# A hand-set order for the first 80 microseconds of a two-layer diffusion trunk

## The chip, the cores and the metric

The kernel runs on one core of one Trainium2 chip. The metric is device time in microseconds (us) for one launch; the time of a kernel is the median of its runs.

## The reference

Two layers work on 512 latent tokens `x` and 256 context tokens `ctx`, each token 1024 wide, all in float32. Only the start matters here:

```python
mod_x = split(silu(c) @ ada_w[0] + ada_b[0], 6)        # shift, scale, gate, ... for x
mod_c = split(silu(c_ctx) @ ada_w[0] + ada_b[0], 6)    # the same for ctx
h_x = rmsnorm(x, norm_g[0, 0]) * (1 + mod_x[1]) + mod_x[0]
h_c = rmsnorm(ctx, norm_g[0, 0]) * (1 + mod_c[1]) + mod_c[0]
p_x, p_c = h_x @ w_in, h_c @ w_in                      # q, k, v of 16 heads in 8 units
q, k = rope(q_x), rope(k_x)                            # latent tokens only
# then scores, softmax, values; output projection; SwiGLU FFN; layer 1; final RMSNorm
```

`rmsnorm(x, g)` is `x * rsqrt(mean(x * x) + eps) * g` over the 1024 features.

## The kernel before

Activations lie transposed: features on the 128 partitions, eight tiles `k = 0..7` of 128 features, tokens along the free dimension. A latent tile is 128x512, a context tile 128x256. Each float32 operand of a large product is split in two parts that TensorE takes at full rate, a high part (rounded by ScalarE) and a low part (the rest, by VectorE); a product is three matmuls, high by high, high by low and low by high (`mm3`). Weights arrive as raw tiles of 128x1024 (512 KB). The class `Stream` holds a list of them in order of use: `S.add` appends, `S.request` issues the loads on SyncE's queue (SP), `S.make` has the parts made, `S.next` hands them out. The pool of raw tiles has three buffers, one more pool at the start ("ada") five; a load waits until its buffer is free.

The start, up to the first attention scores, consists of these steps:

- Loads of `c` (`craw`), of the eight x tiles, and of `c` and `c_ctx` as rows (`crow`); silu of both on ScalarE (the rows are stored again, to be used later).
- The modulation. `ada_w` for shift and scale of the first norm comes in sixteen pieces, eight for features 0 to 511 and eight for 512 to 1023. TensorE multiplies each piece as four small products side by side (`ada_mm`). The sums are copied to SBUF, transposed by TensorE and added to the bias (`ada_out`), which gives `mod` (shift) and `amod` (gain times 1 + scale).
- 1/rms of x: ScalarE squares the tiles, VectorE and GpSimd add the squares into two accumulators (`sq_sum`), TensorE multiplies these with a matrix of ones, and ScalarE and VectorE make the inverse root (`rstd_of`).
- `h_make`: for a tile, VectorE computes x times `amod` times 1/rms, ScalarE adds the shift and rounds (the high part), VectorE makes the low part.
- `part(range(4))`: k, q and V products of unit 0 over tiles 0 to 3; then the second half of the modulation, and `part(range(4, 8))`. The weights are w_ab[8] (k), w_ab[0] (q), w_ab[12] and w_ab[13] (two halves of V).
- The context: its 1/rms, its eight tiles by `h_make`, its k, q and V products (`qk_c`, `v_group`).
- Rope on latent q and k (`rope_of`: a shuffle and a product on VectorE, a product and a sum on GpSimd); evacuation of q and k in two parts for two heads (`evac_pair`); and for k a second tile, k2, in which the halves of the partitions are swapped by two DMAs (`swap_halves`). Scores need k, k2 and q.

`keep_busy` issues small matmuls of `ident` by `ones`, whose results nobody uses.

The order of instructions on each engine is made by the tile framework's planner, which simulates the program and issues on each engine what is ready, in order of program text; `issue_after` pins single instructions. The planner places the loads and parts of later units among all this as buffers become free. Behind the first scores follow five steps of attention for each of eight units, with the projections of the next unit between them as fillers, and then the rest of the two layers.

Of the kernel before, what the change touches and what calls it, by code (L numbers as in the profile page):

```python
# [8 lines left out]
F32 = mybir.dt.float32  # L9
# [23 lines left out]
def f32(ap):  # L33
    return ap.bitcast(F32)
# [3 lines left out]
def tile_trunk(  # L38
# [53 lines left out]
    silu0 = nc.scalar.activation(csil, craw, AF.Silu)  # L92
# [202 lines left out]
    nc.sync.dma_start(tables[0:2, :], crow)  # L295
    with tc.issue_after(silu0.ins):
        silu1 = nc.scalar.activation(tables[0:2, :], tables[0:2, :], AF.Silu)
    nc.sync.dma_start(crow_dram, tables[0:2, :])
    exp_ln_tables(silu1)

# [7 lines left out]
    def rstd_of(ps, accs, dim, pool):  # L308

        n = accs[0].shape[-1]  # L310
        for i, a in enumerate(accs):
            nc.tensor.matmul(ps[:, 0:n], ones, a, start=i == 0, stop=i == len(accs) - 1)
        v = pool.tile([P, n], F32, tag="ns_v", name="ns_v")
# [314 lines left out]
    with ExitStack() as st:  # L628
# [24 lines left out]

        add_ada0(0)
        add_qk(0)
        S.add(w_ab[12])
        add_ada0(1)
        S.add(w_ab[13])
# [6 lines left out]
        with ExitStack() as s0:  # L665
            p0 = s0.enter_context(tc.tile_pool(name="p0", bufs=1, reuse_waits="tile"))
            p1 = PoolMap(ns_v=(p0, "ns_v", 1), ns_y=(p0, "ns_yc", 1), ns_t=(p0, "ns_t", 1))
            S.pools["ada"] = s0.enter_context(tc.tile_pool(name="p0_ada", bufs=5, reuse_waits="tile"))
            S.request(KT)
            nc.gpsimd.dma_start(cost, rope[0, 0])  # L670
            nc.gpsimd.dma_start(sint, rope[0, 1])

            def ada0_mm(b):
                ps = tp()
                for k in range(KT):
                    ada_mm(ps, S.next(0), k, k == 0, k == KT - 1)
                    S.request(min(S.at + 8, 2 * KT + 3))
                return ps

            def ada0_h(b, ps):  # L680
                sb = p0.tile([P, NX], F32, tag="ns_s", name="ada_acc", bufs=2)[:, 0:256]
                nc.vector.tensor_copy(sb, ps[:, 0:256])
                ada_out(sb, tp, [(0, 2, 0, 0, 4 * b), (2, 2, 0, 1, 4 * b)])
                for k in range(4 * b, 4 * b + 4):
                    h_make(k, hx[k], xr[k], rx, 0, 0, 0, p0)

            ps = ada0_mm(0)
            rx = rstd_of(tp(), sq_sum(xr, p0), D, p0)
            ada0_h(0, ps)
            keep_busy(tp(), 10)  # L690
            wk, wq, wv = S.next(), S.next(), S.next()
            psk, psq = linp(), linp()
            psv = [sp2((P, 2, 512)) for _ in range(2)]
            wv = [tuple(wslice(t, 256) for t in wv)]

            def part(ks):
                for ps, w in ((psk, wk), (psq, wq)):
                    wh, wl = (wslice(t) for t in w)
                    for k in ks:
                        nc.tensor.matmul(ps, wh(k), xh(k), start=(k == 0), stop=False)  # L700
                        nc.tensor.matmul(ps, wh(k), xl(k), start=False, stop=False)
                        nc.tensor.matmul(ps, wl(k), xh(k), start=False, stop=(k == KT - 1))
                for t in range(4):
                    c = slice(t * P, (t + 1) * P)
                    for k in ks:
                        wh, wl = wv[k // 4][0](k % 4), wv[k // 4][1](k % 4)
                        a, b = hx[k][:, 0, c], hx[k][:, 1, c]
                        nc.tensor.matmul(psv[t // 2][:, t % 2, 0:256], a, wh, start=(k == 0), stop=False)
                        nc.tensor.matmul(psv[t // 2][:, t % 2, 0:256], b, wh, start=False, stop=False)
                        nc.tensor.matmul(psv[t // 2][:, t % 2, 0:256], a, wl, start=False, stop=(k == KT - 1))  # L710

            for k in range(0, KT, 2):
                nc.sync.dma_start(c2[k // 2].rearrange("p (a b) -> p a b", a=2), ctxT[:, k : k + 2, :])
            part(range(4))
            rc = rstd_of(tp(), sq_sum(cr, p0), D, p1)
            for k in range(4):
                h_make(k, hc[k], cr[k], rc, 0, 0, 1, p0)
            ada0_h(1, ada0_mm(1))
            keep_busy(tp(), 9)
            wv.append(tuple(wslice(t, 256) for t in S.next()))  # L720
            part(range(4, KT))
            for k in range(4, KT):
                h_make(k, hc[k], cr[k], rc, 0, 0, 1, p0)
            del S.pools["ada"]
# [1258 lines left out]
```

## Time and profile before

| | |
|---|---|
| runs of the kernel | 1609.46, 1604.99, 1601.09 us |
| median | 1604.99 us |
| span of the profiled execution, first to last instruction | 1606.8 us |
| mean granted TensorE clock | 0.991 |
| share of the span in which PE, PEld, DVE, ACT, POOL are busy | 96%, 86%, 77%, 46%, 17% |
| first score on PE | 80.23 us after the start |

The page gives the profiled execution by its span alone; it lies between the times of the three runs. In a row of a timeline stand start, duration, engine (PE is TensorE's matmul, PEld its weight load, DVE is VectorE, ACT ScalarE, POOL GpSimd, SP SyncE; a q behind the name is the engine's queue of DMA issues), line in the kernel, operation, what is written from what, shape, count, and in brackets the idle time before it and what ended that. A float32 product with `ones` or `ident` counts as two records. The ends of matmuls are modelled and overlap; the distance of their starts is the time of one.

### The profile page before, as it was taken

How to read it: one execution, taken by the hardware profiler on the slowest of the kernel's cores; microseconds unless marked ns; L12 is line 12 of the kernel's file. 1: busy time of each engine (PE TensorE's matmuls, PEld its weight loads, DVE VectorE, ACT ScalarE, POOL GpSimd, SP SyncE). 2: the span in 40 equal slices, each digit the busy share in tenths (PEclk: the TensorE clock that was granted, in tenths of full speed). 3: DMA queues.
4: the chain of work that ended last, by engine and by line, in shares of the span. 5: the costliest groups of instructions: out<-in, count | busy, mean ns of one | idle time of the engine just before them, and what ended most of it. 6: DMA issues, size and time to landing. Idle time of an engine off the chain costs nothing.

```text
span 1606.8 us, 25479 instructions
## 1 busy us (share of the span) xinstructions
PE 1541.8 (96%) x9854; PEld 1377.4 (86%) x9854; DVE 1242.9 (77%) x2125; ACT 734.1 (46%) x1276; POOL 275.9 (17%) x311
## 2 busy tenths in 40 slices
PE   5899999999999999999999999999998999999997
PEld 3798888877878998999999998886777899989897
DVE  4667798966698789879798867677766987869686
ACT  4346545445344413434424254466664543525354
POOL 2222223463010000010100001354331000000001
PEclk9999999999999999999999999999999999999999
DMA  9312354543145465485866652320011442423321
GB/s 348 100 53 70 99 157 136 182 128 101 63 132 158 118 173 155 133 221 154 213 183 162 201 146 71 106 66 27 15 40 54 131 144 68 131 72 100 118 80 53
DMA packets 68577, 195.28 MB, mean 122 GB/s; under 512 B 6772, under 2 KB 19220, under 8 KB 68456
## 3 DMA queue, kind: packets, MB, share of 16 engines
q1 hardware_dynamic: 58824, 161.26, 31.5%
q0 software_dynamic: 9056, 31.87, 9.4%
q8 instruction: 78, 1.28, 0.3%
q10 hardware_dynamic: 576, 0.52, 0.1%
q14 instruction: 43, 0.35, 0.1%
HBM read 160.45 MB, written 4.86 MB: 103 GB/s over the span
## 4 chain that ended last, share of the span: by engine, by line
PE 52%; DVE 5%; DMA 4%; issue 4%; ACT 1%; POOL 0%; DVEq 0%; POOLq 0%; ACTq 0%; SPq 0%
PE f L1764 4%; PE f L1763 4%; PE f L1762 4%; PE f L1334 4%; PE f L1333 4%; PE f L1332 4%; PE f L1374 3%; PE f L1375 3%; PE f L1373 3%; PE t L411 2%; PE f L1815 2%; PE f L1817 2%; PE f L1816 2%; DMA wl<-raw 2%; PE t L1569 2%
## 5 line engine op out<-in xcount | busy, mean ns | idle before, releaser
L196 ACT ACTIVATE wh<-raw 128x1024 fp32r<-128x1024 f32 (+1 forms) x96 | 92.3, 978 | 232.4 <-DVE raw L540 106.6
L207 PE MATMUL lin<-hb,wh 128*128 128x512 f32 (+1 forms) x456 | 162.1, 356 | 8.3 <-DVE rbuf L387 2.1
L208 PE MATMUL lin<-hb,wh 128*128 128x512 f32 (+1 forms) x456 | 160.3, 351 | 1.0 <-DVE hb L1106 0.7
L209 PE MATMUL lin<-hb,wl 128*128 128x512 f32 (+1 forms) x456 | 158.4, 347 | 0.0
L197 DVE TENSOR_TENSOR wl<-raw,wh 128x1024 fp32r<-128x1024 f32 (+1 forms) x96 | 107.1, 1122 | 36.3 <-ACT wh L196 34.3
L269 DVE SCALAR_TENSOR_TENSOR junk<-raw,tables 128x1024 bf16<-128x1024 f32 x80 | 98.6, 1233 | 19.2 <-DMA raw<-in_ada_wT_dram 18.7
L202 POOL DMA_DIRECT2D wl<-raw x39 | 34.0, 872 | 445.3 <-ACT wl L201 412.0
L207 PEld LDWEIGHTS lin<-hb,wh 128*128 128x128 f32 x456 | 86.3, 189 | 23.9 <-issue 2.8
L1373 PE MATMUL f<-g,wh 128*128 128x512 f32 (+1 forms) x304 | 103.0, 340 | 0.6 <-DVE s L1362 0.6
L1374 PE MATMUL f<-g,wh 128*128 128x512 f32 (+1 forms) x304 | 102.9, 339 | 0.0
L1763 PE MATMUL f<-hb,wh 128*128 128x256 f32 x360 | 101.8, 284 | 0.0
L1762 PE MATMUL f<-hb,wh 128*128 128x256 f32 x360 | 101.6, 283 | 0.0
L1764 PE MATMUL f<-hb,wl 128*128 128x256 f32 x360 | 101.4, 284 | 0.0
L1375 PE MATMUL f<-g,wl 128*128 128x256 f32 (+1 forms) x304 | 100.8, 337 | 0.0
L1334 PE MATMUL f<-hb,wl 128*128 128x384 f32 x288 | 96.5, 335 | 1.0 <-DMA wl<-raw 1.0
L208 PEld LDWEIGHTS lin<-hb,wh 128*128 128x128 f32 x456 | 86.5, 190 | 12.4 <-DVE hb L1106 1.4
L159 DVE TENSOR_TENSOR wl<-raw,wh 128x1024 fp32r<-128x1024 f32 x61 | 80.7, 1325 | 20.6 <-ACT wh L158 20.3
L1332 PE MATMUL f<-hb,wh 128*128 128x384 f32 x288 | 96.4, 335 | 0.0
L1333 PE MATMUL f<-hb,wh 128*128 128x384 f32 x288 | 96.4, 335 | 0.0
L209 PEld LDWEIGHTS lin<-hb,wl 128*128 128x128 f32 x456 | 86.5, 190 | 10.8
L158 ACT CAST wh<-raw 128x1024 fp32r<-128x1024 f32 x61 | 63.9, 1048 | 67.0 <-PE t L208 15.0
L339 POOL TENSOR_TENSOR ns_a<-ns_a,ns_s 128x256 f32<-128x256 f32 (+1 forms) x16 | 17.9, 1118 | 433.7 <-ACT ns_s L335 427.0
(395 smaller groups left out, 4851.3 us busy)
## 6 DMA issues: line engine op xcount, KB each, us to landing
raw<-in_w_dram SPq DMA_DIRECT2D x132, 512.0 KB, 3.7
raw<-in_ada_wT_dram SPq DMA_DIRECT2D x80, 512.0 KB, 3.8
wl<-raw POOLq DMA_DIRECT2D x39, 512.0 KB, 6.3
raw<-in_w_ab_dram SPq DMA_DIRECT2D x24, 512.0 KB, 4.2
raw<-in_ada_w_dram SPq DMA_DIRECT2D x16, 512.0 KB, 9.5
raw<-in_w_c_dram SPq DMA_DIRECT2D x12, 512.0 KB, 4.4
nb<-in_na_bias_dram POOLq DMA_DIRECT2D x16, 256.0 KB, 3.2
raw<-in_wo_ab_dram SPq DMA_DIRECT2D x8, 512.0 KB, 3.7
```

The costliest lines, as they stand in the source:

```text
L207: nc.tensor.matmul(ps, wh(k), xh(k), start=k == 0, stop=False)
L208: nc.tensor.matmul(ps, wh(k), xl(k), start=False, stop=False)
L209: end = nc.tensor.matmul(ps, wl(k), xh(k), start=False, stop=k == n - 1)
L1332: nc.tensor.matmul(ps, wh(k), b[:, 0, :], start=k == 0, stop=False)
L1333: nc.tensor.matmul(ps, wh(k), b[:, 1, :], start=False, stop=False)
L1334: nc.tensor.matmul(ps, wl(k), b[:, 0, :], start=False, stop=k == 3)
L1373: nc.tensor.matmul(ps, hi, g[:, 0, cols[v]], start=first, stop=False)
L1374: nc.tensor.matmul(ps, hi, g[:, 1, cols[v]], start=False, stop=False)
L1375: nc.tensor.matmul(ps, lo, g[:, 0, cols[v]], start=False, stop=last)
L1762: nc.tensor.matmul(ps, wh(k), b[:, 0, :], start=k == 0, stop=False)
L1763: nc.tensor.matmul(ps, wh(k), b[:, 1, :], start=False, stop=False)
L1764: nc.tensor.matmul(ps, wl(k), b[:, 0, :], start=False, stop=k == 3)
```

## The change

From the first load to the first scores every engine now issues in the order of the program text (`manual_schedule` for TensorE, VectorE, ScalarE, GpSimd and SyncE). Where instructions from outside that stretch fall among them is still the planner's choice. The text of the stretch is rewritten:

- Each square of x goes straight to TensorE, eight products with `ones` that accumulate in `psx`. `rstd_from` is the second half of `rstd_of`.
- x times 1/rms is made ahead (`xs`, partly in the tiles that take the context later). When the modulation is there, ScalarE makes the high part from it in one step (`x_hi`), VectorE multiplies and subtracts, and GpSimd adds the shift (`x_lo`).
- The eight ada pieces of the first half follow the squares on TensorE, with six fillers (`busy`) behind each piece from 3 on, and ten behind the transposes. The pieces of the second half stand between the projections of the first.
- Weights are taken raw, and their parts made at set places (`w_hi`, `w_lo`); the parts of w_ab[13] get tiles of their own. The context is loaded after tiles 0 to 3 are done, since it takes their place.
- k and q of the context are multiplied together, tile by tile, and V of the context after them.

```diff
+    by_hand = ExitStack()
+    by_hand.enter_context(tc.manual_schedule(engines={ENG.PE, ENG.DVE, ENG.Activation, ENG.Pool, ENG.SP}))
...
     nc.sync.dma_start(craw, cT)
+    nc.sync.dma_start(tables[0:2, :], crow)
...
+    nc.scalar.activation(csil, craw, AF.Silu)
+    nc.scalar.activation(tables[0:2, :], tables[0:2, :], AF.Silu)
+    nc.scalar.preload_act_table_set("natural_log_exp_and_others")
...
+            S.request(KT)
+            nc.sync.dma_start(crow_dram, tables[0:2, :])
+            S.request(2 * KT + 3)
...
+            for k in range(KT):
+                sq = p0.tile([P, NX], F32, tag="ns_s", name="ns_s", bufs=2)
+                nc.scalar.activation(sq, xr[k], AF.Square)
+                nc.tensor.matmul(psx, ones, sq, start=k == 0, stop=k == KT - 1)
+            rx = rstd_from(psx, NX, D, p0)
...
+            for k in range(4):
+                nc.vector.tensor_mul(scaled(k), xr[k], rx)
...
+            def x_hi(k):
+                nc.scalar.activation(
+                    hx[k][:, 0, :], scaled(k), AF.Identity, bias=mod[0][:, 0, 0, k : k + 1], scale=amod[0][:, 0, 0, k : k + 1]
+                )
+            def x_lo(k):
+                nc.vector.scalar_tensor_tensor(
+                    scaled(k), scaled(k), amod[0][:, 0, 0, k : k + 1], f32(hx[k][:, 0, :]), op0=ALU.mult, op1=ALU.subtract
+                )
+                nc.gpsimd.tensor_scalar(hx[k][:, 1, :], scaled(k), mod[0][:, 0, 0, k : k + 1], 1.0, op0=ALU.add, op1=ALU.mult)
...
+            for k in range(KT):
+                ada0_mm(ps0, k)
+                busy(0 if k < 3 else 6)
+            sb = ada0_copy(ps0)
+            wk, wq, wv0 = (w_tiles(S.next(0)) for _ in range(3))
+            w_hi(wk)
+            ada_out(sb, tp, [(0, 2, 0, 0, 0), (2, 2, 0, 1, 0)])
+            busy(10)
...
+            x_hi(0)
+            w_lo(wk)
+            x_hi(1)
+            w_hi(wq)
+            x_lo(0)
+            x_lo(1)
+            x_hi(2)
+            x_hi(3)
+            w_lo(wq)
+            x_lo(2)
+            x_lo(3)
+            for k in range(0, KT, 2):
+                nc.sync.dma_start(c2[k // 2].rearrange("p (a b) -> p a b", a=2), ctxT[:, k : k + 2, :])
+            S.request(2 * KT + 4)
+            w_hi(wv0)
+            w_lo(wv0)
+            for k in range(4, KT):
+                nc.vector.tensor_mul(scaled(k), xr[k], rx)
+            prods((wk, "hh", lo4), (wk, "lh", lo4), (wq, "hh", lo4), (wk, "hl", lo4), (wq, "hl", lo4), (wq, "lh", lo4))
+            ps1 = tp()
+            ada0_mm(ps1, 0)
...
+            ada0_mm(ps1, 3)
+            v_x(1, wv0, range(4))
+            for k in range(4, KT):
+                ada0_mm(ps1, k)
+            v_x(2, wv0, (0, 1))
+            sb = ada0_copy(ps1)
+            wv1 = w_tiles(S.next(0), p0)
+            w_hi(wv1)
+            ada_out(sb, tp, [(0, 2, 0, 0, 4), (2, 2, 0, 1, 4)])
+            v_x(2, wv0, (2, 3))
+            v_x(3, wv0, range(4))
+            for k in range(4, KT):
+                x_hi(k)
+            for k in range(4, KT):
+                x_lo(k)
+            w_lo(wv1)
+            for k in range(4, KT):
+                prods((wk, "hh", (k,)), (wk, "lh", (k,)), (wq, "hh", (k,)), (wq, "lh", (k,)))
+            prods((wk, "hl", range(4, KT)), (wq, "hl", range(4, KT)))
+            nc.gpsimd.dma_start(cost, rope[0, 0])
+            nc.gpsimd.dma_start(sint, rope[0, 1])
...
+            ropes = [rope_of(ps, z, t) for ps, z, t in ((psk, rp, rt[0]), (psq, PoolMap(ru=(p0, "ns_s", 2)), rt[1]))]
+            v_x(0, wv1, range(4, KT))
+            v_x(1, wv1, range(4, KT))
+            rc = rstd_of(tp(), accs, D, p1)
+            v_x(2, wv1, range(4, KT))
+            v_x(3, wv1, range(4, KT))
+            for k in range(4):
+                h_make(k, hc[k], cr[k], rc, 0, 0, 1, p0)
+            evac_pair(units[0]["k"], NC, NX, ropes[0], 1.0)
+            for k in range(4, KT):
+                h_make(k, hc[k], cr[k], rc, 0, 0, 1, p0)
+            pck, pcq = linp(), linp()
+            for k in range(KT):
+                for ps, w in ((pck, wk), (pcq, wq)):
...
+            evac_pair(units[0]["k"], 0, NC, pck[:, 0:NC], 1.0)
+            swap_halves(units[0]["k2"], units[0]["k"])
+            evac_pair(units[0]["q"], NC, NX, ropes[1], -0.125)
+            evac_pair(units[0]["q"], 0, NC, pcq[:, 0:NC], -0.125)
...
+            v_group(ps, 0, [tuple(wslice(z, 256) for z in w[0:2]) for w in (wv0, wv1)])
...
+        by_hand.close()
```

More of the change, by code (lines that the diff above doesn't have):

```diff
@@ L72, in tile_trunk @@
     dpool = ctx.enter_context(tc.tile_pool(name="dpool", bufs=1, space=bass.MemoryType.DRAM))
+    ENG = mybir.EngineType
+    by_hand = ExitStack()
+    by_hand.enter_context(tc.manual_schedule(engines={ENG.PE, ENG.DVE, ENG.Activation, ENG.Pool, ENG.SP}))
     craw = const.tile([P, KT, 32], F32, name="craw")
+    tables = const.tile([P, 2 * NX], F32, name="tables")
+    cost, sint = tables[:, 0:NX], tables[:, NX : 2 * NX]
     nc.sync.dma_start(craw, cT)
+    nc.sync.dma_start(tables[0:2, :], crow)
     res_tile = lambda: xpool.tile([P, NX], F32, tag="res", name="res", bufs=KT + KT // 2 + 1)
@@ L292, in tile_trunk @@
     exp_ln_tables = lambda after: act_tables("natural_log_exp_and_others", after)
[L295 to L299, printed above, removed]
     def load_rows(cs):
@@ L312, in rstd_of, with rstd_from @@
             nc.tensor.matmul(ps[:, 0:n], ones, a, start=i == 0, stop=i == len(accs) - 1)
+        return rstd_from(ps, n, dim, pool)
+    def rstd_from(ps, n, dim, pool):
         v = pool.tile([P, n], F32, tag="ns_v", name="ns_v")
@@ L652, in add_ada0, with add_raw @@
                 S.add(src[:, :, b * 512 : (b + 1) * 512], "raw" if (k < 3, k > 4)[b] else "ada")
+        def add_raw(j):
+            S.add_made([w_ab[j]], lambda raw: raw[0])
         add_ada0(0)
-        add_qk(0)
-        S.add(w_ab[12])
+        for j in (8, 0, 12):
+            add_raw(j)
         add_ada0(1)
-        S.add(w_ab[13])
+        add_raw(13)
         units, vunits = {}, {}
@@ L664, in tile_trunk @@
         rt = [rbuf[:, 0:NX], rbuf[:, NX : 2 * NX]]
[L665 to L724, printed above, removed]
-            lamt = p0.tile([P, 4, 64], F32, name="lamt")
-            nc.gpsimd.dma_start(lamt, lam4)
-            lprod = p0.tile([P, 2, 64], F32, name="lprod")
-            lsum = p0.tile([P, 2], F32, name="lsum")
-            lv = lamt.rearrange("p (a b) d -> p a b d", b=2)
-            nc.vector.tensor_mul(lprod, lv[:, :, 0, :], lv[:, :, 1, :])
-            nc.vector.tensor_reduce(lsum, lprod, axis=AX.X, op=ALU.add)
-            nc.scalar.activation(lsum, lsum, AF.Exp)
-            nc.vector.scalar_tensor_tensor(
-                neglam, lsum[:, 1:2], -0.2, lsum[:, 0:1], op0=ALU.add, op1=ALU.subtract
-            )
@@ L737, in tile_trunk @@
-        ap = st.enter_context(tc.tile_pool(name="a_work", bufs=2, reuse_waits="tile"))
-        small = lambda name, n: ap.tile([P, n], F32, tag=name, name=name, bufs=4)
-        asml = st.enter_context(tc.tile_pool(name="a_small", bufs=1, reuse_waits="tile"))
         def qk_tiles(u):
@@ L770, in qk_pieces @@
+        by_hand.close()
+        ap = st.enter_context(tc.tile_pool(name="a_work", bufs=2, reuse_waits="tile"))
+        small = lambda name, n: ap.tile([P, n], F32, tag=name, name=name, bufs=4)
+        asml = st.enter_context(tc.tile_pool(name="a_small", bufs=1, reuse_waits="tile"))
         def qk_pieces(u):
@@ L1071, in row_pieces @@
             return out_
-        qk_tiles(0)
-        qk_x(0, "k", psk)
-        qk_x(0, "q", psq)
-        vunits[0] = sp.tile([P, 6, 256], F32, tag="v", name="v")
-        for t in range(2):
-            nc.scalar.copy(vunits[0][:, 2 + 2 * t : 4 + 2 * t, :], psv[t][:, :, 0:256])
-        qk_c(0, "k", [wslice(t) for t in wk])
-        qk_c(0, "q", [wslice(t) for t in wq])
-        ps = linp().rearrange("p (t c) -> p t c", t=2)
-        v_group(ps, 0, wv)
-        nc.scalar.copy(vunits[0][:, 0:2, :], ps)
         def merged(*lists):
```

90 lines of the change are left out of this document (85 added, 5 removed).

## The prediction

> **What bounds the kernel now.** I read the page first, then the busy time by windows, then the timelines of the engines from 0 to 81 us, then the answer for tile k.
>
> ```profile
> span 1606.8 us, 25479 instructions
> 80.00:130.00 50.00, 50.00 (x342) 46.46 (x341) 29.04 (x45) 24.32 (x51) 9.75 (x10) 1.00 0.23 60
> 22.34 0.64 PE L235 MATMUL t<-raw,craw 128*32 128x256 f32 x8 [0.51 <-DMA raw<-in_ada_w_dram]
> 26.61 0.50 PE L700 MATMUL lin<-hb,wh 128*128 128x512 f32 x1 [0.34 <-ACT hb L354]
> 28.80 0.50 PE L701 MATMUL lin<-hb,wh 128*128 128x512 f32 x1 [1.70 <-DVE hb L355]
> 30.92 0.80 PE L700 MATMUL lin<-hb,wh 128*128 128x512 f32 x1 [1.15 <-ACT wh L158]
> 49.71 0.44 PE L243 MATMUL t<-ident,ada_acc 128*128 128x128 f32 x2 [0.62 <-DVE ada_acc L682]
> 80.23 0.28 PE L853 MATMUL s<-k,q 128*128 128x256 f32 x1
> ```
>
> The columns of a window are its length, busy time of PE, PEld, DVE, ACT and POOL, the granted clock, the DMA share and GB/s. From 80 us on PE is busy in all of 50 us, so I take a shift of the first score (80.23) to move the end by as much. Before that, PE finishes the first modulation at 22.34 + 0.64 = 22.98, starts the first projection at 26.61, stalls twice, and transposes the second modulation at 49.71. The page's span is 1.8 us above the median of the three times, 1604.99; I add the change in the span to that median. Half a per cent, 8 us, is about what a measurement of this kernel can tell from no change.
>
> **The new start on PE.** Its prices:
>
> ```profile
> 11.15 1.04 ACT L297 ACTIVATE tables<-tables 2x1024 f32<-2x1024 f32 x1
> 12.21 1.28 ACT L289 ACT_TABLE_LOAD   x1
> 8.06 0.63 ACT L335 ACTIVATE ns_s<-res 128x512 f32<-128x512 f32 x1 [0.81 <-DMA res<-in_xT_dram]
> 2.98 0.42 ACT L92 ACTIVATE craw<-craw 128x256 f32<-128x256 f32 x1 [0.96 <-DMA craw<-in_cT_dram]
> 15.72 3.78 PE L312 MATMUL t<-ns_a,ones 128*128 128x512 f32 x4 [0.41 <-DVE ns_a L341]
> 39.88 1.02 PE L312 MATMUL t<-ns_a,ones 128*128 128x256 f32 x4
> 45.87 3.23 PE L235 MATMUL t<-raw,craw 128*32 128x256 f32 x56
> 49.98 2.17 PE L219 MATMUL t<-ones,ident 128*128 128x128 f32 x18
> ```
>
> On ACT the silu of crow (1.04) and the table load (1.28) move ahead of the squares: craw's silu ends at 3.4, crow lands, by the same 2.2 us as craw, near 3.9, so the first square starts near 6.2 and PE near 6.8. A product of a 512-wide square with ones cost 3.78 / 2 = 1.89 us at the slow rate (two products, two records each) and twice 1.02 / 2, 1.0 us, at the fast one. PE was slow for the whole 3.78 us of that row, so I take two squares slow and six fast: 6.8 + 3.8 + 5.9 = 16.5 us. If warming takes 3 us more it is 18.1. The squares no longer need DVE and POOL adds; those had slack, and the old sums ended on PE at 19.5.
>
> But the eight ada pieces now stand behind all squares, and behind pieces 3 to 7 stand six fillers each. A piece costs 3.23 / 7 = 0.46, a filler 2.17 / 9 = 0.24. The last piece ends at 16.5 + 8 x 0.46 + 4 x 6 x 0.24 = 26.0, against 22.98. The weights are there by then: before, the last of them was waited for until 22.34, with context loads in between that the change moves behind. Then come six fillers (1.4), transposes (0.4) and ten fillers (2.4): first projection at 30.2, 3.6 us later than before. The copy of the sums, the modulation and the first two tiles by ACT fit under these fillers. The scaling of x by 1/rms, four DVE products, and the moves of the small scalings and the crow store cost nothing: DVE waits there for PE. The x halves, w_ab[8], [0] and [12] are loaded long before use.
>
> From 30.2 to the last V product of the context PE has this left: 48 products of 512 at 0.23, 96 of 256 at 0.118, eight ada pieces, two transposes, one sum of squares and 96 context products at 0.12:
>
> ```profile
> 53.71 0.39 PE L700 MATMUL lin<-hb,wh 128*128 128x512 f32 x1
> 53.94 0.40 PE L701 MATMUL lin<-hb,wh 128*128 128x512 f32 x1
> 60.48 0.28 PE L208 MATMUL lin<-hb,wh 128*128 128x256 f32 x1
> 60.60 0.28 PE L209 MATMUL lin<-hb,wl 128*128 128x256 f32 x1
> ```
>
> The starts are 0.23 and 0.12 apart. 11.0 + 11.3 + 3.7 + 0.4 + 1.0 + 11.6 = 39.0 us, so without any wait PE would be through at 69.2, eleven us earlier than the old 80.23. The second modulation is read at about 42 instead of 49; here the change gains 7 us, because ada pieces lie between projections and v products cover the modulation.
>
> **The waits that come instead.** Two follow from the written order.
>
> ```profile
> raw<-in_w_ab_dram SPq DMA_DIRECT2D x14, 512.0 KB, 4.2
> 24.28 1.04 ACT L158 CAST wh<-raw 128x1024 fp32r<-128x1024 f32 x1 [0.57 <-DMA raw<-in_w_ab_dram]
> 43.26 0.88 DVE L353 SCALAR_TENSOR_TENSOR ns_h<-res,amod,ns_y 128x256 f32<-128x256 f32 x2
> 43.78 0.91 ACT L354 ACTIVATE hb<-ns_h,mod 128x256 fp32r<-128x256 f32 x2 [1.47 <-DVE ns_h L353]
> 44.32 0.89 DVE L355 SCALAR_TENSOR_TENSOR hb<-ns_h,mod,hb 128x256 fp32r<-128x256 f32 x2 [0.18 <-ACT hb L354]
> 69.35 1.29 ACT L369 ACTIVATE q<-rbuf 64x512 fp32r<-64x512 f32 x2
> 72.13 1.40 DVE L372 SCALAR_TENSOR_TENSOR q<-rbuf,q 64x512 fp32r<-64x512 f32 x2
> ```
>
> First, w_ab[13] gets its buffer when ada piece 5 of the second half is done (40.9), lands 4.2 us later and is cast by ACT ahead of x_hi(4): 0.1 + 4.2 + 1.04 + 0.6 and hand-overs make 47.7, while the v products that cover it end at 45.5. PE waits 2.2.
>
> Second, context tiles. Before, DVE did two tiles at a time (rows 43.26, 43.78, 44.32), so ACT's turn was hidden: 1.87 for two. In written order each tile is DVE, then ACT, then DVE again: 0.44 + 0.46 + 0.44 and two hand-overs, about 1.48 a tile. PE needs 6 x 0.12 = 0.72 for it and waits 0.76 at each of seven tiles. Between the fourth and fifth tile the k evacuation stands in both queues (1.29 on ACT, 1.40 on DVE), so that one wait is 2.9; with 0.5 for the first tile the stage waits 8.0. So 30.2 + 39.0 + 2.2 + 8.0 = 79.4, which is 0.8 us earlier than before.
>
> Third, POOL against DVE. The low halves of all eight x tiles now end on POOL, and both ropes' four POOL steps come right before and during the context tiles.
>
> ```profile
> 26.00 1.22 DVE L159 TENSOR_TENSOR wl<-raw,wh 128x1024 fp32r<-128x1024 f32 x1
> 66.84 2.21 DVE L159 TENSOR_TENSOR wl<-raw,wh 128x1024 fp32r<-128x1024 f32 x1
> 65.66 0.61 POOL L958 TENSOR_SCALAR nb<-nb 128x512 f32<-128x512 f32 x1 [0.47 <-DMA nb<-in_na_bias_dram]
> 63.91 1.27 POOL L388 TENSOR_TENSOR ru<-ru,tables 128x512 f32<-128x512 f32 x1 [0.17 <-DVE ru L386]
> 66.25 1.71 POOL L389 TENSOR_TENSOR rbuf<-rbuf,ru 128x512 f32<-128x512 f32 x1
> 67.94 1.59 POOL L958 TENSOR_SCALAR nb<-nb 128x512 f32<-128x512 f32 x1
> ```
>
> The DVE subtraction started at 66.84, inside a POOL add that ended at 67.96, and took 2.21 instead of 1.22: it ended 1.1 us after that add. The next POOL step, 0.61 alone, took 1.59 and ended 0.5 after DVE's. They take turns. With turns, POOL's step of 0.61 and the DVE operation it blocks are added one to the other: low halves 0 and 1 reach PE 1.6 late, 6 and 7 2.1 late together, and the context's 1/rms and first tile, behind two shuffles, the table loads (now after the last low half on POOL's queue) and four rope steps of 1.3, 2.2 late; 0.3 more in the tiles. 79.4 + 6.2 = 85.6. Bounds of this term: 0 (no overlap falls badly) and 6.2; I take 6.2, since every overlap in rows 66.84 to 67.94 shows the turn.
>
> Fourth, the clock. PE is busy only about half of 13 us in the context stage.
>
> ```profile
> 26.00:31.00 5.00, 1.81 (x8) 0.83 (x6) 4.51 (x8) 2.77 (x5) 1.77 (x1) 0.88 1.04 391
> 31.00:36.50 5.50, 5.50 (x14) 4.08 (x15) 5.40 (x7) 3.08 (x6) 1.39 (x1) 0.50 1.05 387
> 59.90 0.39 PE L207 MATMUL lin<-hb,wh 128*128 128x256 f32 x1 [1.34 <-DVE rbuf L387]
> 64.44 0.39 PE L207 MATMUL lin<-hb,wh 128*128 128x256 f32 x1 [0.72 <-DVE rbuf L387]
> ```
>
> After 1.81 busy of 5 us the granted clock was 0.50 for 5.5 us; after single waits of 1.34 and 0.72 it stayed. For the 5.8 us of context V products that bounds the cost by 0 and 2.9; half busy lies between, nearer the waits that did nothing, and I take 1.0. The Trainium skill (TensorE: Matmul & The Clock Gate, the table of two states in Part 1) has the clock fall only after a whole idle window of about 3.4 us. By it this term would be 0 and the time 1610; the trace disagrees, since waits of 1.70 and 1.15 sufficed at 28.80 and 30.92.
>
> **Sum.** 85.6 - 80.2 + 1.0 = +6.4 us, 1604.99 + 6.4 = 1611. It assumes that PE meets no wait for k2:
>
> ```profile
> 69.52 0.54 SPq L420 DMA_DIRECT2D k<-k  x1
> 70.11 0.59 SPq L421 DMA_DIRECT2D k<-k  x1
> DMA to landing us min/median/max: 7.6/8.1/8.5
> ```
>
> Before, the swap was issued 10 us ahead of the first score. Now k and q of the context end together and only V products of 5.8 us stand behind: evacuation 2.0, issues 0.6, landing 7.6 make 10.2 us after the k products, so k2 comes 5 us after PE is free. What lies outside the hand-ordered part is still placed by the planner, and 24 products of the next unit's k (5.5 us) would fill it.
>
> **Rivals.** (1) The scores go first in PE's queue and wait for k2: + 5.0, 1616. For it: PE's old order has them directly behind V. Against it: the planner may see the late swap. (2) POOL and DVE hardly meet: 79.4, so 1604 with no clock loss, 1609 with the wait for k2. The rows of 66.84 speak against it. The Trainium skill (SBUF — State Buffer, Who interferes with whom) calls the ports that the two share an exclusive lock, for a DVE instruction with two SBUF inputs against a GpSimd one that reads SBUF; by that rule this rival would have no chance and the time would be 1611, and the trace agrees at both overlaps. (3) Faster: context tiles are ready when PE comes to them, so that the 8.0 of waits vanish and turns do not bite: 30.2 + 39.0 + 2.2 = 71.4, -8.8 us, 1596. Its place is the context stage; it decides once PE's waits there sum below 1 us. The paired rows (0.94 a tile) speak for it, the written order against it. (4) The earlier modulation gains nothing at all at 42 us, fillers and late start included: that would show as transposes at 49 again; it makes (1) worse, and lies inside the upper end.
>
> **How the numbers follow.** Forecast 0.42 (1606 to 1613), rival 1 0.33, rival 2 0.12, rival 3 0.13. The range takes in rivals 1 and 2 and, with 3 us each way for the planner's new order behind the start, reaches 1597 to 1620. Faster by 0.5% (below 1597): 0.13; slower (above 1613): rival 1, 0.33; the rest 0.54.
>
> **What would show it.** PE's last first-half ada piece near 26.0 and first projection near 30; second transposes near 42 to 45; a PE wait of about 2 us before the products of tile 4; context products in steps of 1.5 us with PE idle half the time; DVE or POOL operations of doubled length beside each other; the last context V product at 85, and either u=1 projections or a wait of some 5 us before the first score. The prediction is wrong if the fillers are shorter than 1.4 us, if the context stage is dense, or if the order behind the first score changes by more than the start.

## The result, and the profile after

The changed kernel takes 1611.99 us in the median of six runs (1608.78 to 1613.75), the kernel before 1606.54 on the same chip (six runs, the three shown above among them). The ratio is 1.0039, with an interval of 1.0022 to 1.0056: some 6 us slower. The loss is small, inside half a per cent, but the interval is clear of 1. The forecast was 1611, with a branch of its own from 1606 to 1613. The profiled execution of the changed kernel took 1613.75 us, with a span of 1612.0; before it was 1606.8.

The page:

```profile
span 1612.0 us, 25585 instructions
```

The busy time by windows:

```profile
67.80:74.00 6.20, 5.42 (x24) 4.68 (x24) 4.40 (x9) 2.68 (x5) 0.00 (x0) 0.72 0.08 21
74.00:80.60 6.60, 5.37 (x24) 4.63 (x25) 3.70 (x9) 2.12 (x5) 0.00 (x0) 0.74 0.00 0
80.70:86.40 5.70, 5.70 (x50) 5.70 (x49) 4.80 (x9) 5.55 (x10) 0.14 (x1) 1.00 0.61 141
86.40:130.00 43.60, 43.60 (x300) 40.50 (x299) 26.95 (x43) 21.47 (x49) 12.55 (x15) 1.00 0.29 89
```

The first two rows are the context tiles, the third is the context's V products. The last row is the premise of the prediction. From 86.4 us on PE is busy without a gap, as it was from 80 us on before. So the mark to read is the end of the last V product of the context: below it is called the end of the start. It is 86.32 + 0.12 = 86.44 now and was 80.23 before, 6.2 us later. The span grew by 5.2 and the medians by 5.4; the forecast was +6.4. That 1611 and 1612 lie closer than these is chance, since three more runs moved the median of the kernel before from 1604.99 to 1606.54.

The timeline of PE in that stretch:

```profile
6.25 9.79 PE L719 MATMUL t<-ns_s,ones 128*128 128x512 f32 x16 [6.25 <-ACT ns_s L718]
26.01 0.64 PE L240 MATMUL t<-raw,craw 128*32 128x256 f32 x8
30.39 0.73 PE L775 MATMUL lin<-hb,wh 128*128 128x512 f32 x2
33.72 0.96 PE L775 MATMUL lin<-hb,wh 128*128 128x512 f32 x3 [1.14 <-POOL hb L750]
37.82 0.73 PE L775 MATMUL lin<-hb,wl 128*128 128x512 f32 x2
38.39 1.09 PE L775 MATMUL lin<-hb,wh 128*128 128x512 f32 x4
39.41 0.64 PE L240 MATMUL t<-raw,craw 128*32 128x256 f32 x8
46.49 0.38 PE L248 MATMUL t<-ident,ada_acc 128*128 128x128 f32 x2
50.32 0.50 PE L775 MATMUL lin<-hb,wh 128*128 128x512 f32 x1 [1.29 <-ACT hb L742]
55.64 0.50 PE L775 MATMUL lin<-hb,wh 128*128 128x512 f32 x1 [0.92 <-POOL hb L750]
56.72 1.42 PE L775 MATMUL lin<-hb,wh 128*128 128x512 f32 x5 [0.58 <-POOL hb L750]
60.86 1.02 PE L311 MATMUL t<-ns_a,ones 128*128 128x256 f32 x4
67.80 0.39 PE L866 MATMUL lin<-hb,wh 128*128 128x256 f32 x1 [3.06 <-ACT hb L356]
75.20 0.39 PE L866 MATMUL lin<-hb,wh 128*128 128x256 f32 x1 [1.76 <-ACT hb L356]
86.32 0.28 PE L436 MATMUL t<-wl,hb 128*128 128x256 f32 x1
```

The eight squares run at 6.25 to 16, where PE stood idle before, and the first projection comes at 30.39 instead of 26.61. Then PE waits at just the places that the written order makes: for the low halves from POOL (L750) at 33.72, 55.64 and 56.72, for the high half of tile 4 (L742) at 50.32, and for the first context tile at 67.80.

The timelines of ACT, DVE and POOL show why:

```profile
48.50 1.04 ACT L757 CAST wh<-raw 128x1024 fp32r<-128x1024 f32 x1 [14.64 <-DMA raw<-in_w_ab_dram]
50.30 3.67 DVE L747 SCALAR_TENSOR_TENSOR xs<-xs,amod,hb 128x512 f32<-128x512 f32 x4 [2.82 <-ACT hb L742]
51.14 5.52 POOL L750 TENSOR_SCALAR hb<-xs,mod 128x512 fp32r<-128x512 f32 x4 [13.04 <-DVE xs L747]
60.73 0.69 DVE L389 TENSOR_TENSOR rbuf<-lin,tables 128x512 f32<-128x512 f32 x1 [1.88 <-DMA tables<-in_rope_dram]
64.43 1.38 DVE L323 SCALAR_TENSOR_TENSOR ns_y<-ns_t,ns_y 128x256 f32<-128x256 f32 x1
65.84 1.37 DVE L355 SCALAR_TENSOR_TENSOR ns_h<-res,amod,ns_y 128x256 f32<-128x256 f32 x1
68.19 0.48 DVE L355 SCALAR_TENSOR_TENSOR ns_h<-res,amod,ns_y 128x256 f32<-128x256 f32 x1
```

POOL's four low halves take 5.52 / 4 = 1.38 us each, where another POOL step of that shape took 0.61 without company. A DVE product of a context tile takes 1.37 us beside a rope step on POOL and 0.48 one tile later, when POOL is idle. And the rope's first product on DVE stands 1.88 us for its table, because that load now waits in POOL's queue behind the last low half.

### The profile page after: what moved, and what is told of

It is laid out like the page before. It is cut to its first block, busy times and chain, and to the rows that moved or that the text cites. A ratio compares the mean times of both kernels' runs of the same rounds, so it can differ in the third digit from the quotient of the medians.

```text
span 1612.0 us, 25585 instructions
## 1 busy us (share of the span) xinstructions
PE 1553.2 (96%) x9908; PEld 1383.5 (86%) x9908; DVE 1242.5 (77%) x2123; ACT 734.1 (46%) x1276; POOL 280.0 (17%) x315
## 4 chain that ended last, share of the span: by engine, by line
PE 75%; DVE 10%; DMA 8%; issue 3%; ACT 3%; POOL 1%; SPq 0%; DVEq 0%; ACTq 0%; POOLq 0%
PE f L1451 4%; PE f L1449 4%; PE f L1450 4%; PE lin L212 4%; PE lin L213 4%; PE lin L214 4%; PE f L1881 4%; PE f L1880 4%; PE f L1879 4%; PE t L413 3%; PE f L1491 3%; PE f L1490 3%; PE f L1492 3%; PE f L213 3%; PE f L214 3%
## 5 line engine op out<-in xcount | busy, mean ns | idle before, releaser
L212 PE MATMUL lin<-hb,wh 128*128 128x512 f32 (+1 forms) x440 | 157.3, 358 | 6.5 <-DVE k L382 1.9
L213 PE MATMUL lin<-hb,wh 128*128 128x512 f32 (+1 forms) x440 | 155.1, 353 | 0.5 <-DVE hb L1223 0.5
L214 PE MATMUL lin<-hb,wl 128*128 128x512 f32 (+1 forms) x440 | 153.7, 349 | 0.0
L212 PEld LDWEIGHTS lin<-hb,wh 128*128 128x128 f32 x440 | 83.1, 189 | 21.4 <-issue 2.8
L213 PEld LDWEIGHTS lin<-hb,wh 128*128 128x128 f32 x440 | 83.3, 189 | 11.1 <-DVE hb L1223 0.7
L163 ACT CAST wh<-raw 128x1024 fp32r<-128x1024 f32 x57 | 59.6, 1048 | 58.2 <-PE t L213 15.0
L164 DVE TENSOR_TENSOR wl<-raw,wh 128x1024 fp32r<-128x1024 f32 x57 | 74.0, 1301 | 15.5 <-ACT wh L163 14.8
L341 POOL TENSOR_TENSOR ns_a<-ns_a,ns_s 128x256 f32<-128x256 f32 (+1 forms) x12 | 12.2, 1019 | 420.7 <-ACT ns_s L337 414.1
```

Source lines behind the costliest of these rows:

```text
L212: nc.tensor.matmul(ps, wh(k), xh(k), start=k == 0, stop=False)
L214: end = nc.tensor.matmul(ps, wl(k), xh(k), start=False, stop=k == n - 1)
```

## The experiments

All are changes of the new text unless something else is said. The profile gives the end of the start for one execution; the times are medians, each against the kernel before on the same chip. The last two columns set both against the changed kernel: the end against 86.44, the time as the difference of the ratios times 1605 us.

| kernel | median us | ratio (interval) | end of the start | end, against the change | time, against the change |
|---|---|---|---|---|---|
| the change | 1611.99 | 1.0039 (1.0022 to 1.0056) | 86.44 | | |
| e1, no fillers between pieces | 1608.40 | 1.0033 (1.0020 to 1.0046) | 82.56 | -3.9 | -1.0 |
| e2, context tiles in pairs | 1606.56 | 1.0018 (1.0008 to 1.0028) | 82.38 | -4.1 | -3.4 |
| e3, low halves on DVE | 1607.43 | 1.0027 (1.0016 to 1.0038) | 83.70 | -2.7 | -1.9 |
| e4, new text, planner's order | 1611.14 | 1.0046 (1.0031 to 1.0061) | 85.8 | -0.6 | +1.1 |
| e5, second rope late | 1611.77 | 1.0044 (1.0029 to 1.0059) | 85.51 | -0.9 | +0.8 |
| e6, e1 + e2 + e3 + e5 | 1599.68 | 0.9966 (0.9954 to 0.9978) | 76.75 | -9.7 | -11.7 |
| e7, kernel before + squares on PE | 1612.61 | 1.0047 (1.0031 to 1.0064) | 86.96 | +0.5 | +1.3 |
| e8, e6 + a few fillers | 1600.58 | 0.9972 (0.9960 to 0.9984) | 74.70 | -11.7 | -10.8 |
| e9, e8 + tiles before the weight cast | 1600.58 | 0.9973 (0.9962 to 0.9984) | 72.15 | -14.3 | -10.6 |
| e10, e9 + k evacuation last | 1598.04 | 0.9959 (0.9945 to 0.9974) | 70.98 | -15.5 | -12.8 |
| e11, e3 + e5 | 1607.47 | 1.0013 (1.0003 to 1.0023) | 81.90 | -4.5 | -4.2 |
| e12, rope tables loaded early | 1610.15 | 1.0028 (1.0018 to 1.0037) | 85.04 | -1.4 | -1.8 |

The runs are on several chips, so the ratios are to be compared and not the medians. A ratio is known to some 2 us each way, that of the change to 2.7, so the difference of two to about 3 us. The last two columns go together within 4 us. Most of what the start gains or loses reaches the end; that it does so one to one is not shown. Of the single changes only e2 is clear of that noise in the time, and barely; for the others the end of the start is what tells.

**e1: the fillers between the ada pieces.**

```diff
-                busy(0 if k < 3 else 6)
+                busy(0)
```

> The changed kernel without the six fillers behind each ada piece from 3 on (the ten behind the transposes stay). Theory (the late start and the waits of the written order are paid to the end, one to one): the last piece of the first half, which ended at 26.6, comes when its load does, 20.5 to 22.3; the cast of the k weights, in front of the first tile on ScalarE, started at 24.4 on its load and keeps that, so the first tile is made 3.5 us earlier and the last context V product ends at 82.9 instead of 86.4; time 1608.5. Rival A (the clock falls without the fillers and takes the gain): first projections 0.43 apart, V ends at 85.5 or later, 1611 to 1613. Rival B (the start does not reach the end, the planner's order behind it decides): V ends at 82.9 and the time stays within 2 us of 1612.

PE's timeline in e1:

```profile
22.47 0.64 PE L240 MATMUL t<-raw,craw 128*32 128x256 f32 x8 [0.70 <-DMA raw<-in_ada_w_dram]
27.70 0.71 PE L775 MATMUL lin<-hb,wh 128*128 128x512 f32 x2
```

The pieces now come as their loads land, the first projection 2.7 us and the end of the start 3.9 us earlier. Without the fillers the clock falls for a while: the ten behind the transposes take 3.75 us instead of 2.40. Most of the rest of the 3.9 us is the first wait for low halves, 0.17 instead of 1.14. So the fillers do lie on the path, as the prediction counted them. In the time the gain is not shown: the two intervals overlap for most of their width.

**e2: context tiles two at a time**, as before the change: DVE, DVE, ACT, ACT, DVE, DVE.

```diff
...
-            for k in range(4):
-                h_make(k, hc[k], cr[k], rc, 0, 0, 1, p0)
+            for k in (0, 2):
+                h_pair(k)
             evac_pair(units[0]["k"], NC, NX, ropes[0], 1.0)
-            for k in range(4, KT):
-                h_make(k, hc[k], cr[k], rc, 0, 0, 1, p0)
+            for k in (4, 6):
+                h_pair(k)
```

> The changed kernel with the context tiles made two at a time: VectorE for both, ScalarE for both, VectorE for both. Theory: a tile costs VectorE 0.96 instead of 1.46, eight tiles 4.0 us less, PE's products of the context keep their end behind the last tile, V ends at 82.4 instead of 86.4, time 1608. Rival A (PE itself is the limit there, at half clock 1.4 us for a tile): under 1 us gained, 1611 to 1612. Rival B (the end does not follow the start): V ends at 82.4, time within 2 us of 1612.

PE's context products in e2 as one window, and then the two waits that are left, from the timeline:

```profile
67.67:76.62 8.95, 7.43 (x49) 6.24 (x50) 7.36 (x16) 4.38 (x10) 0.00 (x0) 1.00 0.05 15
```

```profile
67.67 0.39 PE L879 MATMUL lin<-hb,wh 128*128 128x256 f32 x1 [3.25 <-ACT hb L759]
72.95 0.39 PE L879 MATMUL lin<-hb,wh 128*128 128x256 f32 x1 [1.44 <-ACT hb L759]
```

The stage starts where it did (67.67 against 67.80) and takes 8.95 instead of 12.9 us: the turn of one tile on two engines cost 4 us. The granted clock in the stage is 1.00 where the changed kernel had 0.72 and 0.74. This is what rival 3 had as its mechanism; in the changed kernel the written order kept it from happening.

**e3, e5, e11: POOL beside DVE.** e3 puts the add of a low half on DVE. e5 takes the second rope's last two steps from POOL and makes them on DVE after the eight context tiles. e11 does both.

```diff
-                nc.gpsimd.tensor_scalar(hx[k][:, 1, :], scaled(k), mod[0][:, 0, 0, k : k + 1], 1.0, op0=ALU.add, op1=ALU.mult)
+                nc.vector.tensor_scalar(hx[k][:, 1, :], scaled(k), mod[0][:, 0, 0, k : k + 1], 1.0, op0=ALU.add, op1=ALU.mult)
...
-            ropes = [rope_of(ps, z, t) for ps, z, t in ((psk, rp, rt[0]), (psq, PoolMap(ru=(p0, "ns_s", 2)), rt[1]))]
+            ropes = [rope_of(psk, rp, rt[0]), rt[1]]
+            uq = p0.tile([P, NX], F32, tag="ns_s", name="ru", bufs=2)
+            nc.vector.stream_shuffle(uq, psq, mask=SWAP16)
+            nc.vector.tensor_mul(rt[1], psq, cost)
...
+            nc.vector.tensor_mul(uq, uq, sint)
+            nc.vector.tensor_add(rt[1], rt[1], uq)
             pck, pcq = linp(), linp()
```

> The changed kernel with the last step of the low half of the x tiles (the added shift) on VectorE instead of GpSimd. Theory (GpSimd and VectorE take turns): the 1.38 us that GpSimd takes for each tile and the stretched VectorE operations beside it go, PE's three waits for GpSimd's low halves (2.6 us) fall below 1, the table loads of rope no longer stand behind GpSimd's last tile; V ends 1.5 to 3 earlier, at 83.4 to 84.9, time 1609 to 1610.5. Rival (VectorE pays for it itself: eight more operations of 0.4 to 0.7 on the engine that sets the pace): V ends at 86 to 88, time 1611.5 to 1613.5.

> The changed kernel with the second rope's last two steps (for q) on VectorE behind the eight context tiles, instead of on GpSimd before them. Theory (turns of GpSimd and VectorE): the last step of the context's 1/rms (1.38) and the first tile's first step (1.37) fall to 0.42 and 0.48, the first context product comes 1.9 us earlier, V ends at 84.5 instead of 86.4, the ratio to the kernel before falls from 1.0039 to 1.0027. Rival (the start of the context tiles is set by the squares and ScalarE): under 0.5 us.

> The changed kernel with both pieces of work taken off GpSimd: the low halves of x and the last steps of the second rope on VectorE; fillers and single context tiles stay. Theory (turns of GpSimd and VectorE cost what the forecast put there, about 6 of the 86.4): without the second rope beside them the 1.39 and 1.37 of the kernel with low halves on VectorE fall to 0.42 and 0.48, V ends at 81.5 to 82, that is 4.5 to 5 of the 6.2, the rest is VectorE's own eight operations; ratio 1.0005 to 1.002. Rival (the two losses hide one another, or the clock, which fell in the run with the second rope late, decides): V ends at 83.3 or later, ratio 1.0025 or more.

The timelines of PE and DVE in e3, then in e5, then in e11:

```profile
53.42 0.49 DVE L750 TENSOR_SCALAR hb<-xs,mod 128x512 fp32r<-128x512 f32 x1
53.96 1.43 PE L775 MATMUL lin<-hb,wh 128*128 128x512 f32 x5 [0.26 <-DVE hb L750]
61.26 1.39 DVE L323 SCALAR_TENSOR_TENSOR ns_y<-ns_t,ns_y 128x256 f32<-128x256 f32 x1
62.69 1.37 DVE L355 SCALAR_TENSOR_TENSOR ns_h<-res,amod,ns_y 128x256 f32<-128x256 f32 x1
```

```profile
60.80 0.41 PE L789 MATMUL s<-wl,hb 128*128 128x256 f32 x1
61.02 0.41 PE L790 MATMUL s<-wh,hb 128*128 128x256 f32 x1
62.42 1.02 PE L311 MATMUL t<-ns_a,ones 128*128 128x256 f32 x4
65.35 0.42 DVE L323 SCALAR_TENSOR_TENSOR ns_y<-ns_t,ns_y 128x256 f32<-128x256 f32 x1
```

```profile
62.15 0.48 DVE L355 SCALAR_TENSOR_TENSOR ns_h<-res,amod,ns_y 128x256 f32<-128x256 f32 x1
63.23 0.39 PE L871 MATMUL lin<-hb,wh 128*128 128x256 f32 x1 [0.83 <-ACT hb L356]
```

In e3 a low half's add takes 0.49 us on DVE, the waits for low halves shrink from 2.64 in all to 0.26 us, the rope's first product finds its table loaded, and DVE's two operations beside the rope stay at 1.39 and 1.37. In e5 the first of them (L323) is back to 0.42, so the stretch is the work of the second rope on POOL, which was the point. Yet e5 gained only 0.9 us, against 1.9 expected, because in its profiled execution PE's V products ran slowly from 58.2 to 61.4, some 0.21 us apart as in the first two rows, and the context's sum of squares came at 62.42 instead of 60.86. e11 does without both and is at the end of the start where it was expected, 4.5 us earlier, 4.2 in the time.

**e12: the rope tables loaded early**, right after the weights of the start are requested, ahead of the low halves on POOL's queue.

```diff
             S.request(2 * KT + 3)
+            nc.gpsimd.dma_start(cost, rope[0, 0])
+            nc.gpsimd.dma_start(sint, rope[0, 1])
...
-            nc.gpsimd.dma_start(cost, rope[0, 0])
-            nc.gpsimd.dma_start(sint, rope[0, 1])
```

> The changed kernel with the two rope tables loaded at the start of the written stretch instead of behind GpSimd's last low half. Theory: the wait of 1.9 for the table in VectorE's queue goes, rope's GpSimd steps end 1.9 earlier and stretch the context's 1/rms less, V ends 1 to 2 earlier, 84.4 to 85.4. Rival (ScalarE's root and PE's sum come when they came, the turns only move): V ends within 0.5 of 86.4.

DVE's first rope product and PE's first context product in e12:

```profile
58.46 0.67 DVE L389 TENSOR_TENSOR rbuf<-lin,tables 128x512 f32<-128x512 f32 x1
65.80 0.39 PE L866 MATMUL lin<-hb,wh 128*128 128x256 f32 x1 [1.36 <-ACT hb L356]
```

The product has no wait any more and PE reaches the context 2.0 us earlier, of which 1.4 are left at the end of the start.

**e4 and e7: the text without the order, and the squares without the text.** e4 leaves out the one statement that pins the order. e7 is the kernel before with eight squares straight to TensorE, nothing else.

```diff
-    by_hand.enter_context(tc.manual_schedule(engines={ENG.PE, ENG.DVE, ENG.Activation, ENG.Pool, ENG.SP}))
```

> The text of the changed kernel, with the order left to the planner on all engines. Theory (the new text is good for some 7 us at the second modulation, the written order gives it back in the context stage): the planner pairs the context tiles and fills the waits, V ends at 78 to 83, time 1604 to 1608. Rival (the written order is what makes the new text fast, the planner mixes squares, fillers and ada pieces badly): V ends at 87 or later, time 1613 or more.

```diff
-            rx = rstd_of(tp(), sq_sum(xr, p0), D, p0)
+            psx = tp()
+            for k in range(KT):
+                sq = p0.tile([P, NX], F32, tag="ns_s", name="ns_s", bufs=2)
+                nc.scalar.activation(sq, xr[k], AF.Square)
+                nc.tensor.matmul(psx, ones, sq, start=k == 0, stop=k == KT - 1)
+            rx = rstd_from(psx, NX, D, p0)
```

> The kernel before with one part of the change alone: the squares of x go straight to TensorE, the order is the planner's. Theory (1/rms was not late, the first modulation waits for the load of the last ada piece at 22.3): V ends at 79.5 to 81 as before (80.2), the time is the same within 2 us. Rival (the squares stand in front of the ada pieces on PE and delay the modulation): V ends at 82 or later, 1606 to 1609.

PE in e4, then in e7:

```profile
36.10 0.69 PE L247 MATMUL t<-ident,ada_acc 128*128 128x128 f32 x2 [6.39 <-DVE ada_acc L737]
41.46 0.72 PE L774 MATMUL lin<-hb,wh 128*128 128x512 f32 x2
```

```profile
27.23 1.12 PE L695 MATMUL t<-ns_s,ones 128*128 128x512 f32 x2
35.66 1.22 PE L708 MATMUL lin<-hb,wh 128*128 128x512 f32 x2 [3.78 <-ACT hb L357]
```

My theory for e4, that the planner would make more of this text, fell: the first projection comes 11 us later than by hand and the whole is no faster. So the written order is not shown to be worse than the planner's for the same work. My theory for e7, that nothing would change, fell as well; squares in front of ada pieces were its rival. In e7 the planner puts squares and ada pieces on PE by turns; the last square starts at 27.23, and the first projection comes at 35.66, nine us later than in the kernel before. Half of the nine, 4.6, is there at the transposes (28.19 against 23.59), the rest comes behind them, with a wait of 3.78 for ACT. Squares on TensorE are dear in this order; the written order has them in the idle stretch ahead of the pieces.

**e6, e8, e9, e10: versions that gain.** e6 joins e1, e2, e3 and e5. The next three each change one thing in the version before:

```diff
-                busy(0)                    # e8
+                busy(0 if k < 3 else 3)
-            busy(10)
+            busy(8)
...
-            w_hi(wv1)                      # e9: moved behind the loop
             ada_out(sb, tp, [(0, 2, 0, 0, 4), (2, 2, 0, 1, 4)])
...
             for k in range(4, KT):
                 x_hi(k)
+            w_hi(wv1)
...
-            evac_pair(units[0]["k"], NC, NX, ropes[0], 1.0)   # e10: moved behind the tiles
             for k in (4, 6):
                 h_pair(k)
...
+            evac_pair(units[0]["k"], NC, NX, ropes[0], 1.0)
```

> No fillers behind the ada pieces, context tiles in pairs, low halves of x on VectorE and the second rope late, all together. Theory (the four losses lie one behind the other on one chain): 3.9 + 4.0 + 2.7 + 1.9 = 12.5 us less than the changed kernel, V ends at 73.9, the ratio to the kernel before is 0.996. Rival (they hide one another, the loads of weights or VectorE become the limit): V ends at 77 to 79, ratio 0.998 to 0.9995.

> The kernel with all four losses undone, with three fillers behind each ada piece from 3 on (0.72 us, so that piece and fillers stay under the 1.35 us in which the loads come) and eight instead of ten behind the transposes. Theory (without fillers the clock fell: the last pieces took 1.08 and the first projections ran at half rate): the pieces take 0.64 as before, the first projection comes at 26.7 instead of 28.9 and at full rate, V ends 3 to 4 us earlier, at 72.8 to 73.8, ratio 0.9945. Rival (the projections wait for weights and tiles anyway): V ends at 75.5 to 76.8, ratio 0.9955 to 0.997.

> The same, and the cast of w_ab[13] stands behind the four tiles on ScalarE instead of in front of them. Theory: the wait of 1.96 before the products of tile 4 falls below 0.5 and nothing takes its place at once, V ends 1.5 us earlier than without this, ratio 0.9935. Rival (VectorE's low halves and the squares behind them set the pace): 0.5 us or less, ratio as without this.

> The same as the one before it, and the evacuation of the latent k stands behind the eight context tiles instead of between the fourth and the fifth. Theory: the wait of 1.44 at tile 4 of the context goes, V ends 1.4 us earlier; the swap for k2 is issued about as early as before and PE has products of the next unit meanwhile, ratio 0.9925. Rival (k is late now: the evacuation and swap end behind V and the first scores wait, the buffer of the context's k is held longer): the first score with k2 comes no earlier than without this, ratio as without this or higher.

PE in e6, then in e10:

```profile
22.59 1.08 PE L240 MATMUL t<-raw,craw 128*32 128x256 f32 x8 [0.24 <-DMA raw<-in_ada_w_dram]
28.89 1.20 PE L788 MATMUL lin<-hb,wh 128*128 128x512 f32 x2
48.35 0.50 PE L788 MATMUL lin<-hb,wh 128*128 128x512 f32 x1 [1.96 <-ACT hb L742]
```

```profile
70.86 0.28 PE L436 MATMUL t<-wl,hb 128*128 128x256 f32 x1
75.32 0.28 PE L1000 MATMUL s<-k,q 128*128 128x256 f32 x1
```

e6 is 0.34% faster than the kernel before, with the interval clear of 1, though its start ended 2.9 us later than I expected: without fillers the pieces take 1.08 and the first two products 1.20, and the wait before tile 4 has grown to 1.96. The fillers of e8 make the pieces short again (0.64), and the start ends 2.0 us earlier. The order of e9 takes the wait before tile 4 away, 1.37 us in e8. Its start ends 2.5 us earlier, of which 0.5 is there already at the first projection (26.04 against 26.58). The start of e10 ends another 1.2 earlier. e10 is 0.41% faster than the kernel before (interval 0.26% to 0.55%) and 0.8% faster than the change; the intervals of e6, e8, e9 and e10 overlap, so which of them is best is not shown. The ratios expected for e8, e9 and e10, 0.9945 to 0.9925, were all missed: they came at 0.9959 to 0.9973.

What stays open: from e6 to e10 the start ends 5.8 us earlier, while the time falls by 1.1 us, with intervals of two us each way. In e10 the first score follows 4.3 us behind the end of the start, in the changed kernel 0.5 and in e6, e8 and e9 2.8; products of the next unit stand between. Whether the rest is given back there, or the profiled executions lie low among their runs (e8's took 1596.06, its median is 1600.58), these runs don't tell.

## Why the prediction came out

The forecast's own mechanism decided, and rival 1 (scores that wait for k2) did not happen. The steps, each with its measured size, in us; "own work" is what remains of the way from the first projection to the end of the start after all waits:

| step | predicted | measured |
|---|---|---|
| eight squares on PE | 9.7 | 15.97 - 6.25 = 9.7 |
| end of the last ada piece of the first half | 26.0 | 26.58 (its start 26.01) |
| first projection | 30.2 | 30.39 |
| PE's own work from there | 39.0 | 42.0 |
| wait for low halves 0 and 1 | 1.6 | 1.14 |
| wait before tile 4 | 2.2 | 1.29 |
| waits for low halves 6 and 7 | 2.1 | 0.92 + 0.58 = 1.50 |
| wait before the first context tile | 0.5 + 2.2 = 2.7 | 3.06 |
| context tiles, beyond PE's own 5.8 | 7.5 + 0.3 = 7.8 | 80.7 - 67.8 - 5.8 = 7.1 |
| slow clock at the context's V | 1.0 | 0 |
| end of the start | 86.6 | 86.44 |

So the sum is right partly by luck, because errors cancel: PE's work was 3.0 us too short, the waits and the clock together 3.3 us too long. It is the same ahead of the first projection: the squares began 0.5 earlier than forecast, the pieces and fillers behind them took 26.58 - 15.97 = 10.6 instead of 9.5, and what follows the last piece took 3.8 instead of 4.2.

*PE's own work.* I priced every product of 512 at the 0.23 us that the rows of the kernel before showed at 54 us. In the first half they cost more: from 30.39 to 39.98 lie 24 of them, one wait of 1.14 and three ada pieces of 0.57, which leaves 9.59 - 1.14 - 1.71 = 6.74, or 0.28 each (the six of the rows at 37.82 and 38.39 take 1.59); and a single piece between projections costs 0.57, not 0.46. The products are not slower in themselves. Two of them took 36.70 - 36.23 = 0.47 when other products of 512 followed and 37.25 - 36.70 = 0.55 when a piece followed, and the first one behind a wait took 50.65 - 50.32 = 0.33. So what the price left out are the turns: each change from products to a piece and back, and each start behind a wait, adds about 0.1, and the written order has many of them. No run changes the number of turns alone.

*The second modulation.* "Here the change gains 7 us" was too much. The transposes came at 46.49, 3.2 us earlier than the old 49.71, not seven: the products, the wait for low halves and the ada pieces each take a part. That was inside no sum, since own work carries it, but a reader who took the seven us at their word would have expected too much. Rival 4, transposes at 49 again, did not happen.

*Tile 4.* The order did what was said: the cast of the weights stands ahead of the high half on ACT. All of it was some three us late: the cast began at 48.50, not at 40.9 + 0.1 + 4.2 = 45.2, since the ada pieces that free its buffer came later, and the V products that cover it ended at 50.32 - 1.29 = 49.03, not at 45.5. The wait was 0.9 shorter than computed.

*Turns of POOL and DVE.* The prediction took 6.2 us for the turns, its upper bound. e11, without the low halves and the second rope on POOL, gained 4.5, and e12 shows that 1.4 of what I put under this head is the table load that waits in POOL's queue, which I named but did not price by itself. The two are not separate: with the low halves off POOL the table loads come early too, so e11's 4.5 holds that gain too. Taken off whole, it leaves some 3 us for the turns proper, after DVE has paid for the eight adds itself. The Trainium skill (SBUF — State Buffer, Who interferes with whom) calls the ports that the two engines share an exclusive lock, and the lengths here agree: 1.38 against 0.61 on POOL, 1.37 against 0.48 on DVE. Rival 2, that they hardly meet, is refuted by the same rows.

*The clock.* The middle between 0 and 2.9 was wrong for this profile: the context's V products ran at a granted clock of 1.00. The clock did fall within the context tiles (0.72 and 0.74). The products ran up to 0.21 us apart there, so PE was idle for only 2.0 of 12.8 us, not half the time as the prediction had it. This cost next to nothing, since DVE and ACT set the pace: the first product of each tile still started within 0.13 us of the end of its high half on ACT. That the place is open was right; e5 and e6 show it falling at other places. One reading of the kernel before was wrong: the waits of 1.70 and 1.15 did not both bring on its slow stretch, for its clock was 0.50 from 29.79 on, when the second wait had just begun.

*k2.* I took 7.6 us for the landing of the swap. The changed kernel's issue of it on SP's queue and its first product with k2, from the timelines:

```profile
81.77 0.54 SPq L422 DMA_DIRECT2D k<-k  x1
88.99 0.28 PE L983 MATMUL s<-k,q 128*128 128x256 f32 x1
```

and the answer for tile k between 50 and 100 us:

```profile
DMA to landing us min/median/max: 3.8/4.5/5.1
```

It landed in 3.8 to 5.1, and the planner put products of the next unit's k between the scores that need only k (first at 86.9) and those with k2, as the prediction assumed. So the 5 us of rival 1 had no place. In e1, where the first score stands directly behind V, its mechanism does show: PE waits 0.80 us for k2 at 83.64. I gave that rival a third of the chance on one landing time, and that swap was issued at 69.52, right behind a weight load of 512 KB (69.07) and ahead of the next (71.23). In the changed kernel SP issued no weight load between 55.17 and the swap. Over the whole kernel before, the median of eight issues of k halves was 5.0.

*Rival 3* needed dense context tiles. e2 shows that it was right as a mechanism, and worth 4 us of the 8, once the tiles go in pairs.

## What to carry to other kernels

When PE is the bound behind a stretch, price an order written by hand by following the last wait on PE at each place, not by the work it moves: here the squares ran while PE had nothing else to do, but the order written around them made three late arrivals, each a queue position (a cast ahead of a tile, a load behind a low half, DVE and ACT by turns within one tile instead of over two). A hand order is best read as a list of such positions: moving a statement or two took 1.2 to 2.5 us off the start in the profiled executions (e9, e10, e12). And work put on GpSimd beside VectorE cost both: 0.49 us on VectorE was cheaper than 0.61 on GpSimd, which became 1.38.

## What was not expected of the hardware

- The granted clock does not follow from the waits alone. After the same two waits on POOL, 0.92 and 0.58 us, the V products of the changed kernel ran 0.12 us apart, and those of e5, with the same instructions on PE up to there, 0.21 apart for 3.4 us. In these traces the slow stretches that follow a full clock in the start last 3.41 us (58.07 to 61.48 in e5, 69.14 to 72.55 and 75.96 to 79.38 in the changed kernel), twice that (29.79 to 36.62 in the kernel before) or three times (19.95 to 30.19 in e6). Where they can begin differs between executions: laid out in steps of 3.41 us, both waits of e5 fall into one step and those of the changed kernel into two. Two windows of e5, then two of the changed kernel:

```profile
54.65:58.07 3.42, 1.91 (x8) 1.25 (x8) 3.12 (x7) 1.50 (x4) 3.14 (x4) 1.00 0.49 145
58.07:61.48 3.41, 3.41 (x18) 3.41 (x17) 1.30 (x4) 0.00 (x0) 0.00 (x0) 0.50 0.62 167
```

```profile
52.07:55.48 3.41, 2.64 (x12) 1.86 (x10) 3.41 (x4) 1.55 (x5) 3.41 (x3) 1.00 0.00 0
55.48:58.90 3.42, 2.68 (x14) 2.15 (x15) 3.07 (x8) 1.50 (x4) 2.24 (x4) 1.00 0.69 180
```

  PE was busy 1.91 us in the step ahead of e5's slow stretch, 2.64 and 2.68 in those of the changed kernel, which kept its clock. That this share alone decides is not shown: in e2 a step with 1.64 us (62.78 to 66.20) was followed by a clock of 1.00. The Trainium skill (TensorE: Matmul & The Clock Gate, Part 1) has the clock fall only after a whole idle window of about 3.4 us. Neither kernel fits that: in the changed kernel PE was busy 1.24 us in the step ahead of its first slow stretch (65.72 to 69.14).
- The same swap of k halves took 7.6 to 8.5 us to land in the kernel before, between two weight loads, and 3.8 to 5.1 here, where it is issued 12 us later and with no load just ahead.
- With the granted clock at 1.00, PE's products of 512 ran 0.23 us apart in long rows, and each change to another kind of product, or start behind a wait, added about 0.1 us (0.33 from 50.32 to 50.65). Between 30.39 and 39.98 these turns make 0.28 of the 0.23.
